# Sums of squares of the first layer's input taken from feature-major chunks, and a first tile and chunk loaded and split in halves

## The chip, the cores and the metric

The kernel runs on one core of a Trainium2 chip. The metric is the device time of one execution in microseconds (us), as the median of several runs. The engines are named as the profile names them: PE (TensorE, matrix multiplications; PEld is its weight load), DVE (VectorE), ACT (ScalarE), POOL (GpSimd) and SP (SyncE, which here only issues transfers).

## The reference, cut to what matters

Two layers, each over 256 tokens with 2048 features in float32. Everything starts with an RMS norm of the input, whose result goes through one wide projection:

```python
def rms_norm(x, gain):
    xf = x.astype(jnp.float32)
    y = xf * lax.rsqrt(jnp.mean(xf * xf, axis=-1, keepdims=True) + EPS)
    return (y * gain.astype(jnp.float32)).astype(x.dtype)
...
    for layer in range(DEPTH):
        h = rms_norm(x, norm_g[layer])
        proj = jnp.einsum("bsd,de->bse", h, w_in[layer])
        q, k, v, g_att, glu_a, glu_b, g_conv = jnp.split(proj, SPLIT_POINTS, axis=-1)
        q = apply_rope(rms_norm(q.reshape(B, S, N_HEADS, HEAD_DIM), q_norm_g[layer]), cos, sin)
        k = apply_rope(rms_norm(k.reshape(B, S, N_HEADS, HEAD_DIM), k_norm_g[layer]), cos, sin)
...
        conv = conformer_conv(glu_a, glu_b, dw_kernel[layer], dw_bias[layer], conv_ln_g[layer],
                              conv_ln_b[layer], w_pw[layer])
...
        y = jnp.einsum("bse,ed->bsd", jnp.concatenate([att_y, conv_y], axis=-1), w_out[layer])
        x = x + y
```

The factor of a token, one over the root of its mean square, is a number for each row of the projection. The kernel therefore multiplies the plain input (times the gain) with the weights first and applies that factor, `rx`, when a result leaves PSUM.

## The kernel before

**Products.** All wide projections run as one list of groups, one for each 512 output columns. A group is 8 tiles of 256 rows by 512 columns of weights. Every float32 operand is split into a rounded part and a rest: weights from `raw` into `whi` (ACT, line 229) and `wlo` (DVE, line 230), the stationary input into `sthi` (ACT) and `stlo` (DVE). A tile then takes 12 multiplications on PE (two halves of rows, two halves of tokens, three products, lines 616 to 618). Four `raw` buffers are filled by SP in the order of the tiles; a load of tile i+4 waits until the split of tile i has read the buffer. Four buffers hold split tiles, so the split of tile i+4 waits until PE has used tile i.

**Input.** The first layer's input comes feature-major from `x_t` in four chunks `Y[0]` to `Y[3]` (512 features by 256 tokens each), which `first_chunk` splits into `sthi` and `stlo`. Chunk c serves tiles 2c and 2c+1 of every group. The token-major input comes too, in four chunks `A[c]` from `x`, loaded one after another from the list `later`; `x_square` squares each on ACT with a sum along the row, and after the fourth a reduction on DVE and two small operations on POOL (`rsqrt`) give `rx`.

**The rest in between.** Everything that isn't a product is a task of `Filler`: pieces of work that a planner puts between the tiles, by priority and by costs and due times written in the code. The planner runs when the program is built; what it decides is a fixed order of instructions on each engine. The first group is glu_b: its results leave PSUM as `Sigmoid(rx * ps)` on ACT (line 308). The second is glu_a, whose results DVE multiplies with it; PE then transposes the product (line 256), and the convolution starts on DVE. Results of group g-2 have to be out before group g begins.

**POOL's own list.** After the identity matrix POOL issues the load of `mask` and, in `rope_tables`, makes four tables for rotary positions: for each it issues one load of a table and two of a gain row (`gbc`), waits for them, and multiplies (line 588). These are needed first by the group q, after four other groups.

The lines that the change touches, and the start of the program, are these:

Of the kernel before, what the change touches and what calls it, by code (L numbers as in the profile page):

```python
# [16 lines left out]
D = 2048  # L17
# [16 lines left out]
R_RAW, R_SPLIT = 4, 4  # L34
AHEAD = 3

WARM = 14


class Need:  # L40
# [105 lines left out]
def trunk(ctx: ExitStack, tc: tile.TileContext, x, w_in, q_norm_g, k_norm_g, w_pw, w_out, x_t, gains, params,  # L146
# [69 lines left out]
    def load(i):  # L216
        if i >= len(tiles):
            return
        g, s = tiles[i]
        _, _, _, w, row, col, _ = groups[g]  # L220
        r = row + s * KS * 128
        nc.sync.dma_start(raw[i % R_RAW], w[r:r + KS * 128, col:col + CH].rearrange("(k p) c -> p k c", p=128))
        loaded[i] = max(loaded.get(i - 1, 0), halved.get(i - R_RAW, 0) + 2.0) + 1.5

    def split(i):
        if i >= len(tiles):
            return
# [46 lines left out]
    def filled(s, c):  # L274
        vacant[s][c] = False
        ready[s][c] = True

    def first_chunk(c):

        yield Need(A=1.5, V=1.6)  # L280
        p = Y[c].rearrange("p (i s) -> p i s", i=4)
        for i in range(4):
            S.activation(st_hi[0][c][:, i], p[:, i], AF.Copy, scale=ng[:, 4 * c + i:4 * c + i + 1])  # L283
        for i in range(4):
            V.scalar_tensor_tensor(st_lo[0][c][:, i], p[:, i], ng[:, 4 * c + i:4 * c + i + 1],  # L285
                                   st_hi[0][c][:, i].bitcast(F32), op0=ALU.mult, op1=ALU.subtract)
# [7 lines left out]
    def x_square(l, c):  # L294
        yield Need(A=1.4)
        for tt in range(2):
            S.activation(junk, A[c][:, tt], AF.Square, accum_out=ssx[:, tt, c:c + 1])
        flag("x", l, c)
        if all(("x", l, k) in flags for k in range(4)):
            yield Need(V=0.1, G=0.6)  # L300
            V.tensor_reduce(rsc, ssx, axis=mybir.AxisListType.X, op=ALU.add)
            rsqrt(rx, rsc, 1.0 / D, 2)
            flag("rx", l)

    def ev_glu_b(l, j, ps):
        yield Need(0, has("glu", l, j - 1) if j else has("rx", l), A=1.2)
# [55 lines left out]
    def ln_square(l, j):  # L362
        yield Need(V=1.2)
        y = Y[j].rearrange("p (c s) -> p c s", c=4)
        V.tensor_add(y, y, nmean[:, None, :].to_broadcast([128, 4, SEQ]))
        yield Need(0, has("sq", l, j - 2) if j >= 2 else has("rope", l, NCH - 1, "k"), A=1.0)
        sq = Dt[1 + j % 2].rearrange("p t e -> p (t e)")
        S.activation(sq, Y[j], AF.Square)  # L368
        for h in range(2):
            yield Need(0, has("sq", l, j - 1) if j else None, G=1.3)  # L370
            half_sq = sq[:, h * CH:(h + 1) * CH]
            if j == 0 and h == 0:
                G.tensor_copy(ssum, half_sq)
            else:
                G.tensor_add(ssum, ssum, half_sq)  # L375
        flag("sq", l, j)
        if j < NCH - 1:
            return
        yield Need(1, P=0.2)
        ps = fill.bank()  # L380
        for tt in range(2):
            for i in range(2):
                T.matmul(ps[:, 2 * tt:2 * tt + 2], ssum[:, i * SEQ + tt * 128:i * SEQ + tt * 128 + 128],
                         ones[:, :2], start=(i == 0), stop=(i == 1))
        yield Need(V=0.2, G=1.5)
        V.tensor_copy(rsc, ps[:, 0:4:2])
        fill.free(ps)
        rsqrt(rstd, rsc, 1.0 / D, 2)
        G.tensor_copy(rbc, rstd[:, :, None].to_broadcast([128, 2, 128]))
        yield Need(1, P=0.5)  # L390
        ps = fill.bank()
        for tt in range(2):
            T.matmul(ps[:, tt * 128:tt * 128 + 128], rbc[:, tt], ident, start=True, stop=True)
        yield Need(A=0.4)
        S.activation(nmean, ps[:, :SEQ], AF.Copy)
        fill.free(ps)
        for k in range(NCH):
            fill.add(ln_silu(l, k), 4, fill.now[4])
# [162 lines left out]
    for i in range(WARM):  # L561
        T.matmul(acc[3], junk[:, :128], junk, start=True, stop=True)
    S.dma_start(ng, gains)
    S.dma_start(Y[0], x_t[:, 0])
    load(0)
    load(1)
    nc.sync.dma_start(Y[1], x_t[:, 1])
    load(2)
    nc.sync.dma_start(Y[2], x_t[:, 2])
    load(3)  # L570
    later = [(Y[3], x_t[:, 3], None)]
    later += [(A[c], x[0, :, c * CH:(c + 1) * CH].rearrange("(t p) e -> p t e", p=128), c) for c in range(NCH)]
    later.append((prm, params, None))
    make_identity(nc, ident)
    V.memset(half, -0.5)
    V.memset(ones, 1.0)
# [10 lines left out]
                                bass.AP(tensor=src.tensor, offset=src.offset, ap=[[0, 128], [1, 64]]))  # L587
                G.tensor_mul(rope[nm + part], rope[nm + part], gbc[:, None, :].to_broadcast([128, 2, DH]))

    for c in range(NCH):  # L590
        fill.add(first_chunk(c), 0)
    split(0)


    users = {"glu_b": ev_glu_b, "glu_a": ev_glu_a, "v": ev_v, "g_conv": ev_g_conv, "g_att": ev_g_att,
# [3 lines left out]
    for i, (g, s) in enumerate(tiles):  # L599
        l, nm, j, _, _, _, st = groups[g]  # L600
        c = s * KS // 4
        fill.until(lambda: ready[st][c])
        if s == 0 and g >= 2:
            fill.until(has("ev", *groups[g - 2][:3]))
        for a in range(i + AHEAD if i else 1, i + AHEAD + 1):
            split(a)
        ps = [acc[(2 * g + tt) % 4] for tt in range(2)]
        hi, lo = whi[i % R_SPLIT], wlo[i % R_SPLIT]
        order = [(kk, tt) for kk in range(KS) for tt in range(2)]
        if s == NSTEP - 1:  # L610
            order.sort(key=lambda o: o[1])
        for kk, tt in order:
            k = s * KS + kk
            tok = slice(tt * 128, tt * 128 + 128)
            xh, xl = st_hi[st][c][:, k % 4, tok], st_lo[st][c][:, k % 4, tok]
            T.matmul(ps[tt], xh, hi[:, kk], start=(k == 0), stop=False)  # L616
            T.matmul(ps[tt], xh, lo[:, kk], start=False, stop=False)  # L617
            T.matmul(ps[tt], xl, hi[:, kk], start=False, stop=(k == KT - 1))  # L618
        fill.use([("P", 2.6)], halved[i])
        if later and (i == 0 or i % 2):  # L620
            dst, src, c = later.pop(0)
            nc.sync.dma_start(dst, src)
            if c is not None:
                fill.add(x_square(0, c), 3, fill.t["P"] + 4.0)
        if i == NSTEP:
            G.dma_start(mask, log_count)
            rope_tables(0)
        if s % 2 and j == NCH - 1 and nm in last[st]:
            ready[st][c], vacant[st][c] = False, True
        if s == NSTEP - 1:  # L630
            fill.add(users[nm](l, j, ps), 0, fill.t["P"])
            if nm == "o_att" and j == NCH - 1 and l + 1 < DEPTH:
                rope_tables(l + 1)
        fill.run()
# [52 lines left out]
```

## Time and profile before

| what | before |
|---|---|
| median of 3 runs | 1862.9 us (1860.91 to 1862.95) |
| the profiled execution, its own time | 1864.42 us |
| its span in the profile | 1862.6 us |
| busy: PE, DVE, ACT, POOL | 1848.9, 1392.2, 989.0, 139.8 us |
| mean granted clock of PE, as a share of full speed | 0.998 |
| moved by DMA | 352.06 MB, mean 189 GB/s |

The span is the time from the first to the last instruction of the program; the execution's own time has 1.8 us more around it. Busy times of different engines lie beside each other and don't add up to the span.

### The profile page before, as it was taken

To read this page: it belongs to the slowest core of one execution; us is meant where nothing else is said; L and a number is where in the kernel's file an instruction comes from. 1 tells how busy PE (TensorE), PEld (TensorE's weight loads), DVE (VectorE), ACT (ScalarE), POOL (GpSimd) and SP (SyncE) were. 2 spreads that over 40 slices of the span, in tenths; PEclk is the share of its full clock that TensorE was granted. 3 is DMA by queue.
4 is the path that set the end of the run, shared out by engine and by line. 5 is a ranking of instruction groups with operands and counts; after the bars stand their busy time and mean duration, and the time that the engine had idled before them with its cause. 6 is when DMAs were issued, how large, how long until landed. Compare 5 with 4: busy or idle time off the path is not lost.

```text
span 1862.6 us, 23725 instructions
## 1 busy us (share of the span) xinstructions
PE 1848.9 (99%) x8490; PEld 1536.0 (82%) x8490; DVE 1392.2 (75%) x2157; ACT 989.0 (53%) x1559; POOL 139.8 (8%) x153
## 2 busy tenths in 40 slices
PE   8999999999999999999999999999999999999999
PEld 5788888888888888888888888888888888888887
DVE  5678889788889876556558888797887998755554
ACT  5565564554654456445444655646556445644542
POOL 2010100100110141000000101002000102100000
PEclk9999999999999999999999999999999999999999
DMA  8665656656566676556666656565565666666564
GB/s 268 218 184 168 180 179 180 183 167 190 175 179 193 190 225 203 193 189 191 208 203 192 186 162 184 160 197 183 162 183 167 193 194 190 213 204 194 180 204 147
DMA packets 181527, 352.06 MB, mean 189 GB/s; under 512 B 11248, under 2 KB 11248, under 8 KB 181408
## 3 DMA queue, kind: packets, MB, share of 16 engines
q1 hardware_dynamic: 179584, 347.19, 61.3%
q0 software_dynamic: 960, 1.77, 0.6%
q8 instruction: 66, 1.08, 0.2%
q10 hardware_dynamic: 864, 1.59, 0.2%
q14 instruction: 53, 0.43, 0.1%
HBM read 346.31 MB, written 4.19 MB: 188 GB/s over the span
## 4 chain that ended last, share of the span: by engine, by line
PE 97%; DMA 2%; ACT 0%; issue 0%; DVE 0%; SPq 0%; POOL 0%; ACTq 0%; DVEq 0%
PE acc L616 31%; PE acc L618 31%; PE acc L617 31%; PE ax L256 2%; DMA a<-in_x 1%; DMA raw<-in_w_in 1%; PE ax L465 1%; PE ax L482 1%; PE ax L490 0%; PE ax L491 0%; PE ax L489 0%; PE ax L464 0%; DMA y<-in_x_t 0%; ACT whi L229 0%; DVE wlo L230 0%
## 5 line engine op out<-in xcount | busy, mean ns | idle before, releaser
L230 DVE TENSOR_TENSOR wlo<-raw,whi 128x1024 fp32r<-128x1024 f32 x640 | 792.6, 1247 | 413.5 <-ACT whi L229 407.4
L229 ACT ACTIVATE whi<-raw 128x1024 fp32r<-128x1024 f32 x640 | 675.3, 1063 | 657.7 <-PE acc L618 466.3
L616 PE MATMUL acc<-whi,sthi 128*128 128x512 f32 x2560 | 1005.5, 393 | 6.0 <-ACT sthi L283 5.4
L617 PE MATMUL acc<-wlo,sthi 128*128 128x512 f32 x2560 | 997.8, 390 | 2.3 <-DVE wlo L230 2.3
L618 PE MATMUL acc<-whi,stlo 128*128 128x512 f32 x2560 | 998.2, 390 | 0.0
L616 PEld LDWEIGHTS acc<-whi,sthi 128*128 128x128 f32 x2560 | 481.6, 188 | 105.6 <-ACT sthi L283 6.3
L618 PEld LDWEIGHTS acc<-whi,stlo 128*128 128x128 f32 x2560 | 481.2, 188 | 101.5 <-DVE stlo L285 1.0
L617 PEld LDWEIGHTS acc<-wlo,sthi 128*128 128x128 f32 x2560 | 481.6, 188 | 100.9 <-DVE wlo L230 3.2
L339 DVE SCALAR_TENSOR_TENSOR y<-ut,prm,y 128x256 f32<-128x256 f32 x960 | 408.6, 483 | 0.0
L427 POOL TENSOR_SCALAR qr<-qss 128x8 f32<-128x8 f32 x16 | 3.2, 198 | 696.8 <-ACT junk L424 696.8
L347 POOL TENSOR_TENSOR ysum<-ysum,y 128x256 f32<-128x256 f32 x30 | 36.5, 1218 | 240.8 <-DVE y L339 133.5
L424 ACT ACTIVATE junk<-acc,rx 128x128 bf16<-128x128 f32 x128 | 47.1, 368 | 8.4 <-PE acc L618 4.8
L434 ACT ACTIVATE d<-acc,qr 128x128 f32<-128x128 f32 x128 | 34.8, 383 | 15.8 <-POOL qr L429 15.8
L267 ACT ACTIVATE sthi<-ax,prm 128x256 fp32r<-128x256 f32 x64 | 25.1, 476 | 30.7 <-PE ax L256 30.7
L269 DVE SCALAR_TENSOR_TENSOR stlo<-ax,prm,sthi 128x256 fp32r<-128x256 f32 x64 | 26.5, 475 | 14.4 <-ACT sthi L267 14.4
L455 ACT ACTIVATE c<-ax 128x512 f32<-128x512 f32 x32 | 17.4, 596 | 33.6 <-PE ax L256 33.6
L478 ACT ACTIVATE sm<-sm,smm 128x128 f32<-128x128 f32 x64 | 28.2, 443 | 6.6 <-DVE smm L473 6.6
L375 POOL TENSOR_TENSOR ssum<-ssum,d 128x512 f32<-128x512 f32 x14 | 28.5, 2033 | 6.5 <-ACT d L368 5.6
L428 POOL TENSOR_TENSOR qr<-qr,half 128x8 f32<-128x8 f32 x16 | 26.3, 1642 | 1.3
L256 PEld LDWEIGHTS ax<-ident,d 128*128 128x128 f32 x192 | 22.4, 140 | 3.2
L256 PE MATMUL ax<-ident,d 128*128 128x128 f32 x192 | 24.9, 273 | 0.0
L424 ACT ACTIVATION_READ_ACCUMULATOR junk<-acc,rx 128x1 f32 x128 | 24.7, 193 | 0.0
(105 smaller groups left out, 659.3 us busy)
## 6 DMA issues: line engine op xcount, KB each, us to landing
raw<-in_w_in SPq DMA_DIRECT2D x448, 512.0 KB, 4.1
raw<-in_w_out SPq DMA_DIRECT2D x128, 512.0 KB, 4.7
raw<-in_w_pw SPq DMA_DIRECT2D x64, 512.0 KB, 4.6
a<-in_x SPq DMA_DIRECT2D x8, 512.0 KB, 6.0
xs<-a SPq DMA_DIRECT2D x4, 512.0 KB, 6.5
a<-xs SPq DMA_DIRECT2D x4, 512.0 KB, 6.6
y<-in_x_t SPq DMA_DIRECT2D x3, 512.0 KB, 12.4
out<-a SPq DMA_DIRECT2D x4, 256.0 KB, 6.0
```

The lines of the kernel that those rows point to most:

```text
L229: S.activation(hi, a, AF.Copy)
L230: V.tensor_sub(wlo[i % R_SPLIT], a, hi.bitcast(F32))
L256: T.transpose(banks[b][:, i * SEQ + tt * 128:i * SEQ + tt * 128 + 128], src[:, tt, e:e + 128], ident)
L339: V.scalar_tensor_tensor(y[:, c], u[:, c, k:k + SEQ], w[:, c, l * CW + k:l * CW + k + 1], y[:, c], op0=ALU.mult, op1=ALU.add)
L347: G.tensor_add(ysum, ysum, y[:, c])
L375: G.tensor_add(ssum, ssum, half_sq)
L424: S.activation(junk[:, :DH], ps[tt][:, h * DH:(h + 1) * DH], AF.Square, scale=rx[:, tt:tt + 1], accum_out=qss[:, tt, h:h + 1])
L434: S.activation(n[:, tt, h * DH:(h + 1) * DH], ps[tt][:, h * DH:(h + 1) * DH], AF.Copy, scale=qr[:, tt, h:h + 1])
L478: S.activation(s[:, cs], s[:, cs], AF.Exp, bias=m[:, tt:tt + 1], scale=-1.0, accum_out=lsum[:, tt:tt + 1])
L616: T.matmul(ps[tt], xh, hi[:, kk], start=(k == 0), stop=False)
L617: T.matmul(ps[tt], xh, lo[:, kk], start=False, stop=False)
L618: T.matmul(ps[tt], xl, hi[:, kk], start=False, stop=(k == KT - 1))
```

## The change

The first layer's sums of squares are taken from the feature-major chunks, and the token-major input isn't loaded for them. Per chunk, ACT squares 128x1024 numbers into a free buffer (`x_square_first`), POOL adds the two halves into `ssum`, and after the fourth chunk PE multiplies `ssum` with ones (4 small multiplications, `token_sums`), DVE copies two columns, and `rsqrt` follows as before. The four loads of `A` are gone. The first weight tile and the first input chunk are loaded in halves, alternating, all on SP's queue, and split half by half (`split_first`); the first tile's multiplications stand in an order that begins with what comes first. 9 warm-up multiplications stand where 14 stood. The parameters (`prm`) are loaded after tile 7.

```diff
-WARM = 14
+WARM = 9
...
+        src = w[r:r + KS * 128, col:col + CH].rearrange("(k p) c -> p k c", p=128)
+        for kk in range(KS) if i == 0 else [slice(0, KS)]:
+            nc.sync.dma_start(raw[i % R_RAW][:, kk], src[:, kk])
+            if i == 0:
+                x_load(0, 2 * kk, 2 * kk + 2)
...
+    def split_first():
+
+        for kk in range(KS):
+            for k in (2 * kk, 2 * kk + 1):
+                S.activation(*first_hi(0, k), AF.Copy, scale=ng[:, k:k + 1])
+                if k == 2 * kk:
+                    S.activation(whi[0][:, kk], raw[0][:, kk], AF.Copy)
+            V.tensor_sub(wlo[0][:, kk], raw[0][:, kk], whi[0][:, kk].bitcast(F32))
+            for k in (2 * kk, 2 * kk + 1):
+                first_lo(0, k)
+        fill.use([("A", 2.9), ("V", 3.0)], 4.5)
+        halved[0] = 7.0
+        filled(0, 0)
+        fill.add(x_square_first(0), 3, 7.0)
+        load(R_RAW)
...
         filled(0, c)
+        fill.add(x_square_first(c), 3, fill.now[4])
...
+    def x_square_first(c):
+
+        yield Need(0, has("sqx", c - 2) if c >= 2 else None, A=1.0)
+        sq = Dt[1 + c % 2].rearrange("p t e -> p (t e)")
+        S.activation(sq, Y[c], AF.Square)
+        yield from add_squares(sq, c, "sqx")
+        if c == NCH - 1:
+            yield from token_sums()
+            rsqrt(rx, rsc, 1.0 / D, 2)
+            flag("rx", 0)
+
+    def add_squares(sq, j, *name):
+        for h in range(2):
+            yield Need(0, has(*name, j - 1) if j else None, G=1.3)
+            half_sq = sq[:, h * CH:(h + 1) * CH]
+            if j == 0 and h == 0:
+                G.tensor_copy(ssum, half_sq)
+            else:
+                G.tensor_add(ssum, ssum, half_sq)
+        flag(*name, j)
+
+    def token_sums():
+
+        yield Need(1, P=0.2)
+        ps = fill.bank()
+        for tt in range(2):
+            for i in range(2):
+                T.matmul(ps[:, 2 * tt:2 * tt + 2], ssum[:, i * SEQ + tt * 128:i * SEQ + tt * 128 + 128],
+                         ones[:, :2], start=(i == 0), stop=(i == 1))
+        yield Need(V=0.2, G=1.5)
+        V.tensor_copy(rsc, ps[:, 0:4:2])
+        fill.free(ps)
...
-    S.dma_start(Y[0], x_t[:, 0])
     load(0)
     load(1)
-    nc.sync.dma_start(Y[1], x_t[:, 1])
+    x_load(1)
     load(2)
-    nc.sync.dma_start(Y[2], x_t[:, 2])
     load(3)
-    later = [(Y[3], x_t[:, 3], None)]
-    later += [(A[c], x[0, :, c * CH:(c + 1) * CH].rearrange("(t p) e -> p t e", p=128), c) for c in range(NCH)]
-    later.append((prm, params, None))
+    x_load(2)
...
-    for c in range(NCH):
-        fill.add(first_chunk(c), 0)
-    split(0)
+    split_first()
+    for c in range(1, NCH):
+        fill.add(first_chunk(c), 0, 5.0 + 4.0 * c)
...
             split(a)
+            if a == 1:
+                x_load(3)
...
-        if later and (i == 0 or i % 2):
-            dst, src, c = later.pop(0)
-            nc.sync.dma_start(dst, src)
-            if c is not None:
-                fill.add(x_square(0, c), 3, fill.t["P"] + 4.0)
+        if i == NSTEP - 1:
+            nc.sync.dma_start(prm, params)
         if i == NSTEP:
             G.dma_start(mask, log_count)
             rope_tables(0)
```

The planner puts the new work at these places. POOL's list of instructions right behind the identity matrix, before (`gbc` is the gain row of a table):

```order
L626 DMA mask<-in_log_count 128x384
L583 DMA ropeqa<-in_rope_cos 128x2x128
L586 DMA gbc<-in_q_norm_g 128x64 x2
L588 TENSOR_TENSOR ropeqa<-ropeqa,gbc 128x256
L583 DMA ropeqb<-in_rope_sin 128x2x128
```

The same place now (`d_108` and `d_109` hold the squares of chunks 0 and 2, and of 1 and 3):

```order
L351 COPY ssum<-d_108 128x512
L353 TENSOR_TENSOR ssum<-ssum,d_108 128x512
L353 TENSOR_TENSOR ssum<-ssum,d_109 128x512 x2
L353 TENSOR_TENSOR ssum<-ssum,d_108 128x512 x2
L671 DMA mask<-in_log_count 128x384
L627 DMA ropeqa<-in_rope_cos 128x2x128
L630 DMA gbc<-in_q_norm_g 128x64 x2
L632 TENSOR_TENSOR ropeqa<-ropeqa,gbc 128x256
```

The sums of three chunks stand ahead of the mask and the tables now. The end of POOL's tables before, up to the two operations that make `rx`:

```order
L583 DMA ropekb<-in_rope_sin 128x2x128
L586 DMA gbc<-in_k_norm_g 128x64 x2
L588 TENSOR_TENSOR ropekb<-ropekb,gbc 128x256
L247 TENSOR_SCALAR rx<-rsc 128x2
L248 TENSOR_TENSOR rx<-rx,half 128x2
```

The same place now:

```order
L627 DMA ropekb<-in_rope_sin 128x2x128
L630 DMA gbc<-in_k_norm_g 128x64 x2
L632 TENSOR_TENSOR ropekb<-ropekb,gbc 128x256
L353 TENSOR_TENSOR ssum<-ssum,d_109 128x512 x2
L270 TENSOR_SCALAR rx<-rsc 128x2
L271 TENSOR_TENSOR rx<-rx,half 128x2
```

The sum of the fourth chunk stands behind all four tables. PE's list where tile 9 (the second tile of the group glu_a) ends and tile 10 begins, before:

```order
L616 MATMUL acc_156<-whi_94,sthi_65 128x512
L617 MATMUL acc_156<-wlo_98,sthi_65 128x512
L618 MATMUL acc_156<-whi_94,stlo_73 128x512
L616 MATMUL acc_155<-whi_95,sthi_66 128x512
L617 MATMUL acc_155<-wlo_99,sthi_66 128x512
L618 MATMUL acc_155<-whi_95,stlo_74 128x512
```

The same place now:

```order
L665 MATMUL acc_156<-whi_94,sthi_65 128x512
L665 MATMUL acc_156<-wlo_98,sthi_65 128x512
L665 MATMUL acc_156<-whi_94,stlo_73 128x512
L362 MATMUL ax_157<-ones,ssum 128x2 x4
L665 MATMUL acc_155<-whi_95,sthi_66 128x512
L665 MATMUL acc_155<-wlo_99,sthi_66 128x512
```

Four small multiplications, whose operand is POOL's finished `ssum`, stand between the tiles. On ACT `rx` is used at the same place as before: behind the split of tile 13. ACT's list at the start, before, with the semaphores that each row waits for (one of a DMA is named DMAHW; `ng` is the first row's load, of the gains):

```order
L563 DMA ng<-in_gains 128x32
L564 DMA y_81<-in_x_t 128x1024
L229 ACT_TABLE_LOAD
L229 ACTIVATE whi_93<-raw_89 128x1024 [waits DMAHW1_49]
L283 ACTIVATE sthi_65<-y_81,ng 128x256 [waits DMAHW2_49,DMAHW0_49]
```

The same place now:

```order
L611 DMA ng<-in_gains 128x32
L245 ACT_TABLE_LOAD [waits DMAHW2_49]
L245 ACTIVATE sthi_65<-y_81,ng 128x256 [waits DMAHW0_49]
L247 ACTIVATE whi_93<-raw_89 128x512 [waits DMAHW1_49]
L245 ACTIVATE sthi_65<-y_81,ng 128x256
L245 ACTIVATE sthi_65<-y_81,ng 128x256 [waits DMAHW4_49]
```

The load of the activation table comes behind the arrival of the gains, and a quarter of the input chunk is split ahead of the first half of the weights.

## Rows read from the trace of the kernel before

**Rows 1.** Waits of PE over the whole run: us in total, times, longest.

```profile
PE acc L616 <- ACT sthi L283: 5.4, 2, 3.2
```

**Rows 2.** Timeline of PE: start us, us, line, operation [idle before <-releaser].

```profile
9.00 0.55 PE L616 MATMUL acc<-whi,sthi 128*128 128x512 f32 x1 [2.18 <-ACT sthi L283]
...
10.20 0.63 PE L616 MATMUL acc<-whi,sthi 128*128 128x512 f32 x1
...
10.63 0.63 PE L617 MATMUL acc<-wlo,sthi 128*128 128x512 f32 x1
...
19.58 0.80 PE L616 MATMUL acc<-whi,sthi 128*128 128x512 f32 x1 [3.24 <-ACT sthi L283]
...
61.43 0.39 PE L616 MATMUL acc<-whi,sthi 128*128 128x512 f32 x1
...
66.19 0.39 PE L616 MATMUL acc<-whi,sthi 128*128 128x512 f32 x1
...
66.88 1.04 PE L256 MATMUL ax<-ident,d 128*128 128x128 f32 x8
```

**Rows 3.** One stretch: PE, PEld, DVE, ACT, POOL busy, then granted clock, DMA.

```profile
10.00:12.00 2.00, 2.00 (x6) 1.51 (x6) 1.54 (x3) 1.10 (x2) 0.00 (x0) 0.50 0.95 239
```

**Rows 4.** Timeline of POOL, first layer.

```profile
1.43 0.78 POOL L626 DMA_DIRECT2D mask<-in_log_count  x1
...
21.73 0.75 POOL L583 DMA_DIRECT2D ropeka<-in_rope_cos  x1
22.48 1.08 POOL L586 DMA_DIRECT2D gbc<-in_k_norm_g  x2
28.20 0.74 POOL L588 TENSOR_TENSOR ropeka<-ropeka,gbc 128x256 f32<-128x256 f32 x1 [4.64 <-DMA gbc<-in_k_norm_g]
...
36.97 0.73 POOL L588 TENSOR_TENSOR ropekb<-ropekb,gbc 128x256 f32<-128x256 f32 x1 [6.25 <-DMA gbc<-in_k_norm_g]
54.27 0.18 POOL L247 TENSOR_SCALAR rx<-rsc 128x2 f32<-128x2 f32 x1 [16.56 <-DVE rsc L301]
```

**Rows 5.** Timeline of POOL, the last table of the second layer.

```profile
711.82 1.86 POOL L588 TENSOR_TENSOR ropekb<-ropekb,gbc 128x256 f32<-128x256 f32 x1 [3.72 <-DMA gbc<-in_k_norm_g]
```

**Rows 6.** Timeline of ACT, first layer.

```profile
0.72 0.45 ACTq L563 DMA_DIRECT2D ng<-in_gains  x1
...
1.73 1.28 ACT L229 ACT_TABLE_LOAD   x1 [1.73 <-issue]
...
18.07 1.06 ACT L229 ACTIVATE whi<-raw 128x1024 fp32r<-128x1024 f32 x1 [1.53 <-DMA raw<-in_w_in]
19.04 1.69 ACT L283 ACTIVATE sthi<-y,ng 128x256 fp32r<-128x256 f32 x4
20.63 1.04 ACT L229 ACTIVATE whi<-raw 128x1024 fp32r<-128x1024 f32 x1
...
56.45 3.90 ACT L229 ACTIVATE whi<-raw 128x1024 fp32r<-128x1024 f32 x4
```

**Rows 7.** Line 368, ACT's squares for layer_norm: duration ns min/median/max.

```profile
L368 ACT ACTIVATE d<-y x8: 1068/1073/1079, 653.9 to 1588.3; 128x1024 f32<-128x1024 f32 x8
```

**Rows 8.** Instructions on `ssum`, both layers: duration ns min/median/max.

```profile
L383 PE MATMUL ax<-ones,ssum x16: 166/251/251, 679.9 to 1601.3; 128*128 128x2 f32 x16
L375 POOL TENSOR_TENSOR ssum<-ssum,d x14: 1296/2154/2168, 655.7 to 1591.7; 128x512 f32<-128x512 f32 x14
L373 POOL COPY ssum<-d x2: 614/616/617, 655.0 to 1575.8; 128x512 f32<-128x512 f32 x2
```

**Rows 9.** DMA: issues by line (KB, us to landing), then the landing of `gbc`.

```profile
ng<-in_gains ACTq DMA_DIRECT2D x1, 16.0 KB, 3.8
...
DMA to landing us min/median/max: 3.2/5.0/10.2
```

**Rows 10.** Timeline of DVE in the second layer's first normalisation, POOL adding squares beside it.

```profile
652.60 1.22 DVE L230 TENSOR_TENSOR wlo<-raw,whi 128x1024 fp32r<-128x1024 f32 x1
...
656.66 4.55 DVE L230 TENSOR_TENSOR wlo<-raw,whi 128x1024 fp32r<-128x1024 f32 x2
```

More of the change, by code (lines that the diff above doesn't have):

```diff
@@ L221, in load, with x_load @@
         r = row + s * KS * 128
-        nc.sync.dma_start(raw[i % R_RAW], w[r:r + KS * 128, col:col + CH].rearrange("(k p) c -> p k c", p=128))
+        src = w[r:r + KS * 128, col:col + CH].rearrange("(k p) c -> p k c", p=128)
[3 more added lines that the diff above has]
+                x_load(0, 2 * kk, 2 * kk + 2)
         loaded[i] = max(loaded.get(i - 1, 0), halved.get(i - R_RAW, 0) + 2.0) + 1.5
+    def x_load(c, a=0, b=4):
+        nc.sync.dma_start(Y[c][:, a * SEQ:b * SEQ], x_t[:, c, a * SEQ:b * SEQ])
     def split(i):
@@ L276, in filled, with first_hi, first_lo @@
         ready[s][c] = True
+    def first_hi(c, i):
+        return st_hi[0][c][:, i], Y[c][:, i * SEQ:(i + 1) * SEQ]
+    def first_lo(c, i):
+        hi, src = first_hi(c, i)
+        V.scalar_tensor_tensor(st_lo[0][c][:, i], src, ng[:, 4 * c + i:4 * c + i + 1], hi.bitcast(F32),
+                               op0=ALU.mult, op1=ALU.subtract)
     def first_chunk(c):
         yield Need(A=1.5, V=1.6)
-        p = Y[c].rearrange("p (i s) -> p i s", i=4)
         for i in range(4):
-            S.activation(st_hi[0][c][:, i], p[:, i], AF.Copy, scale=ng[:, 4 * c + i:4 * c + i + 1])
+            S.activation(*first_hi(c, i), AF.Copy, scale=ng[:, 4 * c + i:4 * c + i + 1])
         for i in range(4):
-            V.scalar_tensor_tensor(st_lo[0][c][:, i], p[:, i], ng[:, 4 * c + i:4 * c + i + 1],
-                                   st_hi[0][c][:, i].bitcast(F32), op0=ALU.mult, op1=ALU.subtract)
+            first_lo(c, i)
         filled(0, c)
+        fill.add(x_square_first(c), 3, fill.now[4])
     def x_chunk(l, c):
@@ L368, in ln_square @@
         S.activation(sq, Y[j], AF.Square)
[L369 to L376, printed above, removed]
+        yield from add_squares(sq, j, "sq", l)
         if j < NCH - 1:
             return
[L379 to L387, printed above, removed]
+        yield from token_sums()
         rsqrt(rstd, rsc, 1.0 / D, 2)
@@ L611, in trunk @@
             order.sort(key=lambda o: o[1])
-        for kk, tt in order:
+        products = [(kk, tt, n) for kk, tt in order for n in range(3)]
+        if i == 0:
+            products.sort(key=lambda o: (o[0], o[2]))
+        for kk, tt, n in products:
             k = s * KS + kk
@@ L615, in trunk @@
             xh, xl = st_hi[st][c][:, k % 4, tok], st_lo[st][c][:, k % 4, tok]
-            T.matmul(ps[tt], xh, hi[:, kk], start=(k == 0), stop=False)
-            T.matmul(ps[tt], xh, lo[:, kk], start=False, stop=False)
-            T.matmul(ps[tt], xl, hi[:, kk], start=False, stop=(k == KT - 1))
+            T.matmul(ps[tt], xl if n == 2 else xh, lo[:, kk] if n == 1 else hi[:, kk],
+                     start=(k == 0 and n == 0), stop=(k == KT - 1 and n == 2))
         fill.use([("P", 2.6)], halved[i])
-        if later and (i == 0 or i % 2):
-            dst, src, c = later.pop(0)
-            nc.sync.dma_start(dst, src)
-            if c is not None:
-                fill.add(x_square(0, c), 3, fill.t["P"] + 4.0)
+        if i == NSTEP - 1:
+            nc.sync.dma_start(prm, params)
         if i == NSTEP:
```

## The prediction

> **What bounds the kernel now.** I read the waits of PE first. Over the whole run PE waits for other engines only a few times; the largest sum is 5.4 us in two waits, for the split input [rows 1]. Then I read PE's timeline to see where its waits lie: all before 60 us. The first product starts at 9.00, a second wait of 3.24 us ends at 19.58, and at 66.88 stand the first transposes [rows 2]. From there to the end PE has work without a gap, so whatever moves 66.88 moves the end by as much, and the case is decided before it.
>
> At full clock a product follows the one before it every 0.2267 us: from 61.43 to 66.19 there are 21 steps [rows 2]. Seventeen tiles of 12 products stand ahead of the transposes: 204 x 0.2267 = 46.25 us. 66.88 - 9.00 - 46.25 = 11.6 us are lost behind the first product, and 9.00 us ahead of it. That is all that an edit of the start could win. After a pause the products are slower: 10.20 and 10.63 lie 0.43 us apart [rows 2], and the granted clock of that stretch is 0.50 [rows 3], the lower of the two levels, 1.2 GHz. Eight such products cost 8 x 0.2 = 1.6 us more.
>
> The third view is POOL's timeline. POOL does one thing after another: a table for rotary positions takes 0.75 for its load's issue, 1.08 for the two gain rows' issue, 4.64 waiting for them and 0.74 for the multiplication, 7.2 us in all, and the four of them and the mask keep POOL from 1.43 to 37.7 us [rows 4]. Before, that delays nobody: `rx` is asked of POOL at 54.27 only, after 16.56 us of idleness [rows 4].
>
> **The change part by part.**
>
> *The first halves.* The activation table's load, which ran at 1.73, stands behind the arrival of the gains now: issued at 0.72 [rows 6], landed 3.8 us later [rows 9], at 4.5; with the 1.28 us of the load [rows 6] ACT begins at 5.8. A quarter of the input chunk (a fourth of 1.59, the step of four, 19.04 to 20.63 [rows 6]) and half a weight tile (between 0.4, the step of a 256-column quarter, and 0.97, a fourth of the 3.90 that four full ones take [rows 6]; I take 0.6, half and something fixed) give a first product at 6.8 instead of 9.00: 2.2 us won. The five warm-up products that are gone end earlier in a time when PE waits anyway; if the clock starts lower for it, that is within the 1.6 us, which I leave as they are.
>
> *The third tile.* Before, ACT came to the split of tile 3 when its weights landed at 18.07 [rows 6], the seventh of seven half-megabyte loads; the second chunk was split behind it, and so PE waited until 19.58. Now it is the sixth, and POOL's loads are no longer beside it. A sixth or seventh of the way less gives 0.7 + 17.3 x 6/7 = 15.6; without POOL's loads I take 14.5, bounds 13 and 18. PE would wait about 1 us where it waited 3.24.
>
> *The squares.* The four loads of `A`, their eight squarings and the wait for the last are gone, and `rx` would be early. In exchange ACT does four squares of 1.07 us [rows 7] and POOL eight operations on `ssum`. What matters is where POOL does the last two. The order shows the sums of chunks 0 to 2, then the mask and all four tables, then the sum of chunk 3; and on PE the four multiplications of `ssum` between tiles 9 and 10. PE takes its products in the order of its list, so tile 10 and all behind it wait for POOL's tables. The sum for that:
>
> 1. ACT from tile 3's split (14.5) to the end of chunk 2's square: five weight splits, three chunks and two squares lie ahead (5 x 0.97 + 3 x 1.59 + 2 x 0.98 = 11.6), then the square itself, 1.07: 27.2.
> 2. POOL adds chunk 2: two operations. Before, such an addition takes 2.154 us in the median and 1.296 at least [rows 8]. DVE splits weights at the time, so I take the median: 31.5. The earlier chunks' sums (0.62 for the copy, 2.15 each otherwise) fit between the squares.
> 3. The mask's issue, 0.78 [rows 4]: 32.3.
> 4. Four tables. Two at 7.2 as above, while loads still run; two at 6.3, with the shortest wait that a table had, 3.72 [rows 5], since by about 45 us every buffer is full and SP's loads stop. Together 27.0: 59.3. Bounds: with the shortest landing of a gain row, 3.2 [rows 9], less its 0.54 of issue, all four take 4 x (0.75 + 1.08 + 2.7 + 0.73) = 21.0; with the longest late wait, 6.25 [rows 4], 4 x 8.8 = 35.
> 5. The two additions of chunk 3. By then DVE has nothing to split, for tile 14 needs a buffer that PE's tile 10 frees. I take the least duration, 2 x 1.30 = 2.6; with the median it would be 4.3: 61.9.
> 6. Four multiplications with ones, 0.25 [rows 8] and their weight loads: 0.9. Tile 10 begins at 62.8.
> 7. Seven tiles to the transposes: 84 x 0.2267 = 19.04, and 1.6 for the clock after so long a pause: 83.4.
>
> That is 83.4 - 66.88 = 16.5 us later. `rx` itself (a copy, a small power) comes some 4 us after the sums, and ACT needs it only when PE comes to tile 14, 10.9 us on: hidden. PE would have come to tile 10 by about 15 + 8 x 2.72 = 37 to 39, so its wait there is some 23 us.
>
> On step 5 the additions' two durations matter. In the second layer, while POOL adds squares, two of DVE's subtractions take 4.55 us where one alone takes 1.22 [rows 10]: both are slowed. The Trainium skill (SBUF — State Buffer, "SBUF: two separate sides") says that an operation of DVE with two inputs and one of GpSimd exclude each other at a shared port for a whole instruction. The trace agrees, with 2.28 for 1.22. By this rule the squares on POOL would also slow DVE's splits between 17 and 31 us, against the change; by the rows about (2.28 - 1.22) x 6 = 6 us of DVE's time, whose share on PE ends before 40 us, inside the wait for POOL.
>
> *What costs nothing.* `prm` is loaded later, but the convolution that reads it begins after the transposes. The longer list of ACT (four squares for eight squarings) is shorter in time. Were the wait for POOL gone, DVE's slowing would show with up to some 4 us.
>
> **The sum.** Span: 1862.6 + 16.5 = 1879.1. The profiled execution took 1.8 us more than its span, 1864.42; it was slower than the median of the runs, 1862.9. I put the change on the median: 1879.4, so 1879.
>
> **The rivals.**
>
> *The change does what it says, and the tables are not in the way.* Were `ssum` ready when PE comes to tile 10, the losses behind a first product at 6.8 would be the clock (1.6), the third tile (1.0), DVE beside POOL (2.0, half of its up to 4) and the small multiplications (0.9): 6.8 + 46.25 + 5.5 = 58.6 at the transposes, 8.3 us earlier: 1855. For that the four tables would have to be done by 34. Their issues and multiplications alone, without any wait, take 0.78 + 4 x 2.56 = 11.0 us from 31.5 on, so with the order as it is this would need chunk 2 squared some 10 us earlier too. Break-even is tile 10 at about 46.2, with `ssum` whole at 45.3; the least of all bounds (step 1 at 25.7, additions of 1.3, tables of 21.0) gives 52.7. Chance 0.04; no change 0.02.
>
> *The tables are quick in the quiet.* With waits of 2.7 throughout, tile 10 begins at 56.8 and the time is 1873. If the waits in the quiet were shorter still, 1870. For it: SP's loads stop. Against: in neither layer is a wait under 3.72 seen. Chance 0.10 for under 1873. The Trainium skill (DMA: Bandwidth & Descriptors, "Anatomy of one DMA — SWDGE (gpsimd) path") gives a fixed cost of about 2.0 us for a small transfer of this kind. By that the estimate is waits of about 1.5 us after the last issue and some 1868; no row here shows one so short.
>
> *The tables are slow.* At 8.8 each and late weights at the start (18 in step 1): 8 + 3.5 more, 1891. For it: the last table of the first layer waited 6.25 beside SP's loads. Chance 0.08 for more than 1887.
>
> **How the numbers follow.** The forecast, a wait for POOL with tables between the bounds, has 0.76 within 1873 to 1887; the low end is taken down to 1871 since the quiet case is the likelier of the two tails. A change under 0.2% (3.7 us) can't be told from none by such runs. All cases but the first rival are slower by more: slower 0.94, same 0.02, faster 0.04.
>
> **What the profile of the changed kernel would show.** Right: the largest wait of PE is that of the multiplications with ones for POOL's `ssum`, once, 20 to 26 us; POOL's last two additions begin behind the fourth table, near 59, and take about 1.3 us each; the first product stands near 6.8, the third tile's near 15. Wrong: if that wait is under 8 us, POOL's sums were earlier than the order says, and the first rival holds; if the wait is as said but the transposes lie under 78, step 4's waits were too long; if PE has new waits after 83 us, the shift isn't the whole of it.

## The result, and the profile after

| what | before | after |
|---|---|---|
| median (4 runs each, on the same chip) | 1862.9 us (1860.91 to 1864.51) | 1880.9 us (1879.75 to 1882.54) |
| the profiled execution, its own time | 1864.42 us | 1879.75 us |
| its span | 1862.6 us | 1878.0 us |
| mean granted clock of PE | 0.998 | 0.994 |
| moved by DMA | 352.06 MB | 349.97 MB |

The changed kernel takes 1.0095 of the time before (95% interval 1.0082 to 1.0108). It is slower by 0.8 to 1.1%, 18.0 us by the medians and 15.4 us by the two profiled spans.

The first view is again the waits of PE: engine, line, what it waited for, then us in total, times, and the longest. After the change:

```profile
PE ax L362 <- POOL ssum L353: 20.9, 1, 20.9
PE acc L610 <- DVE junk L608: 1.4, 1, 1.4
PE acc L665 <- ACT whi L247: 1.2, 1, 1.2
PE acc L665 <- DVE wlo L237: 1.2, 1, 1.2
PE acc L665 <- DVE stlo L306: 0.5, 1, 0.5
```

One wait of 20.9 us leads the list. It is that of the multiplications with ones for POOL's `ssum`, and it comes once. The 5.4 us for the split input [rows 1] are gone; in their place stand 1.2 at the first product and 0.5 at the third tile.

The second view is PE's timeline after the change, at the places of [rows 2]:

```profile
6.70 1.22 PE L665 MATMUL acc<-whi,sthi 128*128 128x512 f32 x2 [1.24 <-ACT whi L247]
...
15.16 0.50 PE L665 MATMUL acc<-whi,stlo 128*128 128x512 f32 x1 [0.47 <-DVE stlo L306]
...
30.04 0.50 PE L665 MATMUL acc<-wlo,sthi 128*128 128x512 f32 x1 [1.22 <-DVE wlo L237]
...
37.91 0.39 PE L665 MATMUL acc<-whi,stlo 128*128 128x512 f32 x1
59.16 1.86 PE L362 MATMUL ax<-ones,ssum 128*128 128x2 f32 x8 [20.87 <-POOL ssum L353]
60.89 0.77 PE L665 MATMUL acc<-whi,sthi 128*128 128x512 f32 x1
...
64.87 0.52 PE L665 MATMUL acc<-whi,sthi 128*128 128x512 f32 x1
...
82.06 1.04 PE L279 MATMUL ax<-ident,d 128*128 128x128 f32 x8
```

The first product is 2.3 us earlier, the third tile's wait (tile 2, as tiles are counted from 0) is 0.47 us where it was 3.24, and PE is done with ten tiles at 38.3. Then it stands for 20.9 us, and the transposes begin at 82.06 where they began at 66.88.

What POOL did meanwhile, in its own timeline (first layer):

```profile
20.59 7.99 POOL L353 TENSOR_TENSOR ssum<-ssum,d 128x512 f32<-128x512 f32 x4 [2.44 <-ACT d L339]
28.51 0.78 POOL L671 DMA_DIRECT2D mask<-in_log_count  x1
29.30 0.74 POOL L627 DMA_DIRECT2D ropeqa<-in_rope_cos  x1
30.03 1.11 POOL L630 DMA_DIRECT2D gbc<-in_q_norm_g  x2
38.37 0.72 POOL L632 TENSOR_TENSOR ropeqa<-ropeqa,gbc 128x256 f32<-128x256 f32 x1 [7.24 <-DMA gbc<-in_q_norm_g]
...
45.45 0.72 POOL L632 TENSOR_TENSOR ropeqb<-ropeqb,gbc 128x256 f32<-128x256 f32 x1 [4.59 <-DMA gbc<-in_q_norm_g]
...
50.66 0.72 POOL L632 TENSOR_TENSOR ropeka<-ropeka,gbc 128x256 f32<-128x256 f32 x1 [2.71 <-DMA gbc<-in_k_norm_g]
...
55.83 0.72 POOL L632 TENSOR_TENSOR ropekb<-ropekb,gbc 128x256 f32<-128x256 f32 x1 [2.68 <-DMA gbc<-in_k_norm_g]
56.52 2.59 POOL L353 TENSOR_TENSOR ssum<-ssum,d 128x512 f32<-128x512 f32 x2
```

Three chunks are summed at 28.5. The mask and the four tables then hold POOL until 56.5, and only behind them stand the last two additions, 2.6 us of work for which PE has been waiting since 38.3. Of those 28 us POOL spends 17.2 in four waits for gain rows.

Stretches of the same execution (their length, then PE, PEld, DVE, ACT and POOL busy, the granted clock, the share of DMA, GB/s) show how the stop spreads:

```profile
40.00:50.00 10.00, 0.00 (x0) 0.00 (x0) 2.62 (x3) 3.05 (x3) 3.36 (x6) 0.56 0.85 255
50.00:60.00 10.00, 0.84 (x4) 0.84 (x5) 0.00 (x0) 0.00 (x0) 5.69 (x7) 0.50 0.12 20
60.00:70.00 10.00, 10.00 (x36) 8.27 (x37) 1.65 (x3) 3.39 (x4) 0.91 (x2) 0.74 0.07 8
```

From 50 to 60 us ACT and DVE do nothing either, all split tiles and `raw` buffers being full, so the loads stop too (20 GB/s). The granted clock has fallen to 0.50 by then, and PE pays for it behind the wait.

### The profile page after: what moved, and what is told of

The parts are those of the page before. It is cut to its first block, busy times and chain, and to the rows that moved or that the text cites. A ratio compares the mean times of both kernels' runs of the same rounds, so it can differ in the third digit from the quotient of the medians.

```text
span 1878.0 us, 23730 instructions
## 1 busy us (share of the span) xinstructions
PE 1848.6 (98%) x8493; PEld 1537.6 (82%) x8493; DVE 1397.2 (74%) x2158; ACT 987.5 (53%) x1548; POOL 151.7 (8%) x161
## 2 busy tenths in 40 slices
DMA packets 180599, 349.97 MB, mean 186 GB/s; under 512 B 11216, under 2 KB 11216, under 8 KB 180480
## 4 chain that ended last, share of the span: by engine, by line
PE 97%; DMA 1%; POOL 1%; ACT 0%; issue 0%; SPq 0%; DVE 0%; POOLq 0%
PE acc L665 91%; PE ax L279 2%; PE ax L513 1%; DMA gbc<-in_q_norm_g 1%; PE ax L530 1%; POOL ssum L353 1%; DMA raw<-in_w_in 0%; PE ax L538 0%; PE ax L539 0%; PE ax L537 0%; PE ax L512 0%; DMA gbc<-in_k_norm_g 0%; PE ax L362 0%; POOL gbc L630 0%; ACT whi L236 0%
## 5 line engine op out<-in xcount | busy, mean ns | idle before, releaser
L290 ACT ACTIVATE sthi<-ax,prm 128x256 fp32r<-128x256 f32 x64 | 25.1, 475 | 30.7 <-PE ax L279 30.7
L353 POOL TENSOR_TENSOR ssum<-ssum,d 128x512 f32<-128x512 f32 x21 | 40.1, 1908 | 9.3 <-ACT d L431 5.6
L526 ACT ACTIVATE sm<-sm,smm 128x128 f32<-128x128 f32 x64 | 28.2, 442 | 6.6 <-DVE smm L521 6.6
L279 PE MATMUL ax<-ident,d 128*128 128x128 f32 x192 | 24.9, 273 | 0.0
```

Source lines behind the costliest of these rows:

```text
L279: T.transpose(banks[b][:, i * SEQ + tt * 128:i * SEQ + tt * 128 + 128], src[:, tt, e:e + 128], ident)
L526: S.activation(s[:, cs], s[:, cs], AF.Exp, bias=m[:, tt:tt + 1], scale=-1.0, accum_out=lsum[:, tt:tt + 1])
```

## The experiments

Every kernel was timed beside the kernel before on the same chip, and that one's median was 1862.7 to 1863.2 us on each of them. One table first, since it holds for all. The third number column is the 27th product, the first that needs the remainders of the second chunk; the last is the span less the moment of the first transposes.

| kernel | median us | first product | 27th product | transposes | span from there |
|---|---|---|---|---|---|
| before | 1862.9 | 9.00 | 20.84 | 66.88 | 1795.7 |
| after | 1880.9 | 6.70 | 15.16 | 82.06 | 1795.9 |
| e1, tables last | 1857.6 | 6.77 | 15.24 | 59.21 | 1795.9 |
| e2, tables' loads at once | 1870.4 | 6.82 | 16.03 | 72.73 | 1796.0 |
| e3, ones behind tile 13 | 1872.1 | 6.91 | 15.36 | 75.80 | 1795.9 |
| e4, halves alone | 1861.0 | 7.61 | 18.25 | 64.28 | 1795.6 |
| e5, squares, whole start | 1857.1 | 7.97 | 15.63 | 58.12 | 1796.0 |
| e6, e1 and later squares | 1854.8 | 6.78 | 15.90 | 57.29 | 1795.9 |
| e7, e6 and 14 warm-ups | 1854.7 | 7.11 | 15.83 | 57.24 | 1796.0 |
| e8, e5 and later squares | 1855.0 | 8.06 | 15.39 | 56.80 | 1796.0 |

From the first transposes to the end all ten take 1795.6 to 1796.0 us. The case is decided ahead of that point, and each difference of medians can be looked for there.

**e1: the tables behind tile 16.** Theory: POOL's tables ahead of its last sum are the whole loss. The rival is that something else of the change (squares beside splits, ones on PE) costs as well.

```diff
-        if i == NSTEP:
+        if i == 2 * NSTEP:
             G.dma_start(mask, log_count)
             rope_tables(0)
```

> Edit: the mask and the four tables are issued after tile 16 instead of tile 8, so that on POOL they stand behind all sums of squares and behind rx; nothing else differs from the changed kernel. Theory (PE waits in its own list for POOL's sums, and POOL's sums wait for the tables): the 20.9 us wait goes away entirely, tile 10 begins near 39, the transposes stand at 58 to 59.5 and the median is 1853 to 1857, faster than before the change. Rival (the squares are late for another reason: ACT's list, or POOL's additions beside DVE): the wait shrinks only in part, the transposes stay above 66.9 and the median above 1862.

Measured: 1857.6 us, 0.9972 of before (0.9961 to 0.9982). PE's timeline of e1:

```profile
31.20 0.50 PE L665 MATMUL acc<-wlo,sthi 128*128 128x512 f32 x1 [2.29 <-DVE wlo L237]
...
39.26 0.95 PE L362 MATMUL ax<-ones,ssum 128*128 128x2 f32 x8
...
59.21 1.04 PE L279 MATMUL ax<-ident,d 128*128 128x128 f32 x8
```

The multiplications with ones wait for nothing, and take 0.95 us at full clock. The place of the tables alone is worth 23.3 us, and makes of a loss a gain. It is more than the wait of 20.9 us, for with the wait the slow clock behind it goes as well. That it came out 0.6 us above the range points at the one wait that is left, 2.29 us for a split by DVE at tile 7. POOL's and DVE's timelines of e1 lie beside each other there:

```profile
20.67 11.62 POOL L353 TENSOR_TENSOR ssum<-ssum,d 128x512 f32<-128x512 f32 x6 [2.45 <-ACT d L339]
```

```profile
23.09 5.85 DVE L306 SCALAR_TENSOR_TENSOR stlo<-y,ng,sthi 128x256 fp32r<-128x256 f32 x4
28.86 6.78 DVE L237 TENSOR_TENSOR wlo<-raw,whi 128x1024 fp32r<-128x1024 f32 x4
```

Four remainders that take 1.66 us elsewhere take 5.85 while POOL adds squares. ACT had split tile 7's weights at 22.98; DVE came to them at 28.86 only, so it was DVE that PE waited for. e6 asks whether POOL's additions are the cause.

**e2: the tables' loads issued in one go.** Theory: the time in the tables is waiting, row by row; with a buffer for each gain row the twelve loads wait together. They stay ahead of the last sum.

```diff
-                G.dma_start(rope[nm + part], tab.rearrange("(t p) d -> p t d", p=128))
...
-                G.tensor_mul(rope[nm + part], rope[nm + part], gbc[:, None, :].to_broadcast([128, 2, DH]))
+        for (n, g, tab, swap), gbc in zip(todo, gbcs):
+            G.dma_start(rope[n], tab.rearrange("(t p) d -> p t d", p=128))
...
+        for (n, g, tab, swap), gbc in zip(todo, gbcs):
+            G.tensor_mul(rope[n], rope[n], gbc[:, None, :].to_broadcast([128, 2, DH]))
```

> Edit: the tables stay ahead of the fourth chunk's sum, but have a gain row's buffer each; all twelve loads are issued in a row and the four multiplications follow. Theory (the tables cost what their four waits one behind the other cost): POOL needs 0.8 + 7.3 for issues, one wait of 5 to 8 us and 2.9 for the multiplications, 16 to 19 instead of 27.4 us; PE's wait falls from 20.9 to 10 to 13 us and the median to 1869 to 1873. Rival (the wait comes from something other than the tables, or POOL's loads go one after another anyway): the median stays within 2 us of 1881.

Measured: 1870.4 us, 1.0038 (1.0024 to 1.0052). POOL's timeline of e2:

```profile
30.17 0.74 POOL L629 DMA_DIRECT2D ropeqa<-in_rope_cos  x1
...
37.07 0.71 POOL L629 DMA_DIRECT2D ropekb<-in_rope_sin  x1 [1.48 <-DMA gbc<-in_q_norm_g]
...
46.52 0.72 POOL L635 TENSOR_TENSOR ropekb<-ropekb,t 128x256 f32<-128x256 f32 x1 [1.52 <-DMA t<-in_k_norm_g]
47.20 2.60 POOL L354 TENSOR_TENSOR ssum<-ssum,d 128x512 f32<-128x512 f32 x2
```

The tables take 17.0 us in place of 27.2, and PE waits 10.7 in place of 20.9: us for us. What went is waiting: POOL's waits in the tables (three of them at issues, three at multiplications) come to 6.7 us, where they were 17.2, while issues and multiplications take about 10 us in either kernel.

**e3: the ones later on PE.** Theory: it is the place of the multiplications with ones in PE's list that turns POOL's lateness into PE's. POOL is left as it is; PE may do tiles 10 to 13 first.

```diff
-        yield Need(1, P=0.2)
+        yield Need(1, lambda: tile_now[0] >= 13, P=0.2)
```

> Edit: POOL's list as in the changed kernel, tables included; only the multiplications with ones stand behind tile 13 on PE instead of tile 9. Theory (what costs is PE's own list, not that rx is late): the sums are ready at the same 59 us, PE does four more tiles (10.9 us) ahead of them, its wait falls from 20.9 to about 10, the transposes stand near 71 and the median is 1869 to 1872. Rival (a late rx holds up the first group's way out on ACT, whatever PE's list): the wait turns up elsewhere on PE and the median stays within 3 us of 1881.

Measured: 1872.1 us, 1.0046 (1.0032 to 1.006). PE's largest wait of e3, then POOL's last additions:

```profile
PE ax L363 <- POOL ssum L354: 13.9, 1, 13.9
```

```profile
54.51 0.72 POOL L633 TENSOR_TENSOR ropeka<-ropeka,gbc 128x256 f32<-128x256 f32 x1 [5.08 <-DMA gbc<-in_k_norm_g]
...
60.62 2.59 POOL L354 TENSOR_TENSOR ssum<-ssum,d 128x512 f32<-128x512 f32 x2
```

The direction is as expected, the size is not: since PE goes on, the weights' loads go on as well (from 50 to 55 us 216 GB/s are moved, 39 in after), the third table waits 5.08 where it waited 2.71, and the last additions begin at 60.62 where they began at 56.52. Four microseconds of the gain are given back.

**e4: the halves alone.** The start in halves, with the token-major input and the tables as before.

```diff
-        fill.add(x_square_first(0), 3, 7.0)
-        fill.add(x_square_first(c), 3, fill.now[4])
+    later = [(A[c], x[0, :, c * CH:(c + 1) * CH].rearrange("(t p) e -> p t e", p=128), c) for c in range(NCH)]
+    later.append((prm, params, None))
```

> Edit: only the first half of the change: first tile and chunk in halves, 9 warm-up products; the squares come from the token-major input as before, with its four loads after tiles 1, 3, 5 and 7, and the tables run on POOL from the start as before. Theory (the start gains by itself and the squares on POOL lose): first product near 6.8, transposes at 59 to 63, median 1855 to 1859. Rival (the start's gain is eaten, since the chain of four loads of A and their squares sets rx): transposes at 65 to 67, median 1861 to 1863.

Measured: 1861.0 us, 0.9988 (0.9979 to 0.9997), under 0.2% from before. ACT's timeline of e4:

```profile
15.48 1.06 ACT L236 ACTIVATE whi<-raw 128x1024 fp32r<-128x1024 f32 x1 [0.28 <-DMA raw<-in_w_in]
...
30.05 0.63 ACT L325 ACTIVATE junk<-a 128x512 bf16<-128x512 f32 x1 [4.17 <-DMA a<-in_x]
...
47.79 0.63 ACT L325 ACTIVATE junk<-a 128x512 bf16<-128x512 f32 x1 [2.31 <-DMA a<-in_x]
```

The time lies between the two. The start wins 2.6 us at the 27th product (18.25 for 20.84), as much as tile 3's weights are split earlier (15.48 for 18.07 [rows 6]), and all of it is still there at the transposes, against the rival. It is no more for two reasons that the table and these rows show. POOL's loads stay in the start: the first product comes at 7.61, not near 6.8 as expected, and tile 3's split at 15.48 (6.70 and 12.39 in after). And ACT goes on standing in its list for the four loads of `A`, 11.8 us in four waits of which the first and the last are shown; behind such stops come PE's five waits between 32 and 57 us, 3.4 us in all.

**e5: the squares with the start as before.** First tile and chunk whole, 14 warm-ups, feature-major squares, tables last.

```diff
-WARM = 9
+WARM = 14
...
-    split_first()
-    for c in range(1, NCH):
-        fill.add(first_chunk(c), 0, 5.0 + 4.0 * c)
+    for c in range(NCH):
+        fill.add(first_chunk(c), 0)
+    split(0)
```

> Edit: only the second part of the change, with the tables out of the way: the start is that of before (first tile whole, first chunk whole on ACT's queue, 14 warm-up products), the squares come from the feature-major chunks, and mask and tables are issued after tile 16. Theory (start and squares gain apart from each other, and what they gain adds up less than fully, since the four loads of A hold tiles 11 to 14 whatever the start does): first product at 8 to 9, second chunk's tile near 17 since POOL's loads are gone from the start, transposes at 61 to 63, median 1857.5 to 1860. Rival (the gain of the kernel with the tables last is the start's): transposes at 65 to 67, median 1861 to 1863.

Measured: 1857.1 us, 0.9968 (0.9956 to 0.998). That is e1's time without the halves: beside the squares the halves add nothing, against the theory, and the transposes come at 58.12, earlier than the 61 to 63 expected. The reason is in the arrival of the weights of tile 3, behind whose split ACT has the second chunk's, in ACT's timeline of e5:

```profile
12.86 1.06 ACT L233 ACTIVATE whi<-raw 128x1024 fp32r<-128x1024 f32 x1 [1.58 <-DMA raw<-in_w_in]
```

Before it stood at 18.07 [rows 6], with the same order of loads on SP's queue and the same list on ACT up to there. What is gone from the start is POOL's table loads. The stretch from 10 to 15 us, first before and then in e5, shows it in the last column (GB/s) at the same share of DMA:

```profile
10.00:15.00 5.00, 5.00 (x17) 3.95 (x17) 1.90 (x3) 1.10 (x2) 1.17 (x2) 0.73 0.97 327
```

```profile
10.00:15.00 5.00, 4.69 (x19) 3.01 (x17) 3.49 (x3) 3.27 (x6) 0.00 (x0) 1.00 1.03 383
```

e4 and after are the second such pair: both start in halves, e4 with POOL's tables beside it and after without, and tile 3's weights are split at 15.48 and 12.39.

**e6: the squares 10 us later.** Theory: POOL's additions slow DVE's splits of the start; planned later, they meet DVE when it has slack.

```diff
-        fill.add(x_square_first(0), 3, 7.0)
+        fill.add(x_square_first(0), 3, 7.0 + 10.0)
...
-        fill.add(x_square_first(c), 3, fill.now[4])
+        fill.add(x_square_first(c), 3, fill.now[4] + 10.0)
```

> Edit: the kernel with the tables last, and every chunk's square is due 10 us later to the planner, so that ACT's squares stand one to two tiles later and the multiplications with ones behind tile 11 instead of 9. Theory (the 2.3 us that PE still waits at tile 7 come from POOL's additions beside DVE's subtractions): that wait goes or falls under 1 us, DVE's four remainders of the fourth chunk take 1.7 to 4 instead of 5.85 us, and the median is 1854.5 to 1857.5. Rival (that wait is for late weights, or the contention only moves to the next tiles): another wait of 1 to 3 us appears and the median stays at 1857 to 1859.

Measured: 1854.8 us, 0.9954 (0.9942 to 0.9967). DVE's and POOL's timelines of e6:

```profile
22.15 1.66 DVE L306 SCALAR_TENSOR_TENSOR stlo<-y,ng,sthi 128x256 fp32r<-128x256 f32 x4
```

```profile
28.82 10.84 POOL L353 TENSOR_TENSOR ssum<-ssum,d 128x512 f32<-128x512 f32 x6 [2.09 <-ACT d L339]
```

The last chunk's remainders take 1.66 us again, tile 7's wait is gone, and the transposes come 1.9 us before e1's. POOL's additions still slow DVE, but later, where it has idle time between its splits, and PE doesn't wait for it there; alone such a split takes 1.22:

```profile
30.47 2.12 DVE L237 TENSOR_TENSOR wlo<-raw,whi 128x1024 fp32r<-128x1024 f32 x1 [1.49 <-ACT whi L236]
```

**e7 and e8: what the start is worth now.** e7 is e6 with 14 warm-ups in place of 9; e8 is e5 with the later squares of e6, the whole start of before.

```diff
-WARM = 9
+WARM = 14
```

> The changed kernel with tables last, squares planned 10 us later, and 14 warm-up products as before the change, in place of 9. Theory (PE's start is paced by the arrival and the split of the third and fourth weight tile, so a first product 1.2 us earlier or a higher clock in the first 12 products only lengthens the wait at that tile): the product with the third tile's remainders stands at 15.2 to 16.0 as with 9 warm-ups, the transposes at 56.5 to 57.8, the median at 1854 to 1856, not to be told from the 1854.8 of the same kernel with 9. Rival (the warm-ups end at about 7.5, behind the moment when the first half is split, so they delay the first product by 0.7 us and all that follows with it): transposes at 58, median 1855.5 to 1856.5.

> The start of the kernel before (first tile and chunk whole, 14 warm-ups) with feature-major squares planned 10 us later and the tables last. Theory (the halves win nothing that PE can keep, because the third tile's chunk is split at about 15 in either; feature-major squares, the tables' place and the squares' time make all of the gain): first product near 8.0, the third tile's remainders at 15.2 to 16.2, transposes at 56.5 to 58, median 1854 to 1856. Rival (the halves are worth their 1.2 us once nothing else waits): transposes 1 to 1.5 us later than with halves, median 1856 to 1857.5.

Measured: e7 1854.7 us, 0.9955 (0.9943 to 0.9968); e8 1855.0 us, 0.996 (0.9947 to 0.9974). Both theories hold. PE's timeline of e8:

```profile
8.06 0.50 PE L659 MATMUL acc<-whi,sthi 128*128 128x512 f32 x1 [1.39 <-ACT sthi L310]
...
15.39 0.50 PE L659 MATMUL acc<-whi,stlo 128*128 128x512 f32 x1 [0.53 <-DVE stlo L303]
```

Its first product is 1.3 us behind that of e6, its 27th is not behind at all: all of them meet at the third tile, whose chunk comes behind tile 3's weights and isn't split before about 15. e6, e7 and e8 can't be told apart, and all three are faster than the kernels before and after the change.

## Why the prediction was right, point by point

The forecast was 1879 (1871 to 1887), slower, and 1880.9 was measured. Its mechanism is the one that the profile shows, and e1 to e3 take it apart: without the tables ahead of the last sum the loss is gone, with shorter tables it shrinks by as much, and with the ones later on PE it shrinks. That the number came so near is in part luck, since several terms were off and their errors cancel.

*The first halves.* First product at 6.8 forecast, 6.70 measured. The term for the gains was luck: I took them for what holds up the table's load, at 4.5. They landed 3.0 us behind their issue, at 3.7; the load waited for the first half of the input chunk, and ran at 4.32:

```profile
4.32 1.28 ACT L245 ACT_TABLE_LOAD   x1 [4.32 <-DMA y<-in_x_t]
```

In e4, where the gains landed as early but that half later, it ran at 5.23. The first eight products stand 0.43 us apart or a little more, and from the first to the 27th 2.1 us are lost beside the wait of 0.47; I had kept 1.6 for that.

*The third tile.* ACT came to it at 12.39, not 14.5, outside my bounds of 13 to 18: POOL's loads in the start had cost more than I gave them, 5.2 us (e5) where I took 1.1 off for them. That tile 3's weights are the sixth load and no longer the seventh is worth nothing: as the seventh, in e5, they are split at 12.86, as the sixth, in e6, at 13.13. PE's wait was 0.47 for 1.

*Steps 1 and 2.* The timeline of ACT after the change has tile 3's split and the square of chunk 2 at:

```profile
12.39 1.06 ACT L236 ACTIVATE whi<-raw 128x1024 fp32r<-128x1024 f32 x1 [0.28 <-DMA raw<-in_w_in]
...
23.84 1.05 ACT L339 ACTIVATE d<-y 128x1024 f32<-128x1024 f32 x1
```

The square ends at 24.9 (27.2 forecast), 12.5 us behind the start of tile 3's split as in the sum (12.7). The three chunks' sums were done at 28.5 and not 31.5: 2.3 us of that are the earlier square, the rest the additions. Of POOL's row of four the first, of chunk 1, takes 3.67 us, and chunk 2's two are done 3.7 us behind their square, where I took 2 x 2.154 [rows 8].

*Steps 3 and 4.* From the mask's end to the last table 27.2 us; 27.0 forecast. The sum was right and its parts were not, so it was right by luck. I took two tables of 7.2 and two of 6.3; they took 9.7, 7.1, 5.2 and 5.2. The first, beside the weights' loads, waited 7.24 us. The kernel before has a longer one, for its own first table, which I had left out as belonging to the crowded start, and that was the mistake:

```profile
13.83 0.74 POOL L588 TENSOR_TENSOR ropeqa<-ropeqa,gbc 128x256 f32<-128x256 f32 x1 [9.78 <-DMA gbc<-in_q_norm_g]
```

The last two waited 2.7, the value of the quiet rival and of my lower bound. The first two took 2.4 us more than the sum has, the last two 2.2 less, and the errors cancel. The price of the Trainium skill (DMA: Bandwidth & Descriptors, "Anatomy of one DMA — SWDGE (gpsimd) path"), about 2.0 us fixed, by which I had estimated waits of 1.5 us and 1868, was too low here: in the quietest stretch, at 20 GB/s, the wait behind the last issue was still 2.68 us, and no landing of a gain row was under 3.0:

```profile
DMA to landing us min/median/max: 3.0/4.4/7.6
```

*Step 5.* Two additions alone: 2.59 for 2.6.

*Step 6.* The multiplications with ones took 1.86 us for 0.9. The price was that of full clock, which e1 confirms (0.95 at a granted clock of 1.00); here PE had stood for 20 us and the granted clock was 0.50, and behind the waits of e2 and e3 they took 1.87. Half the clock for the small multiplications is the term that I left out.

*Step 7.* Nine products stand 0.43 us apart or more until 64.87, so that the pause cost some 2 us of clock, 1.6 forecast. The transposes came at 82.06 for 83.4, the shift was 15.2 us for 16.5.

*The wait* was 20.9 us, forecast at 20 to 26. Behind 82 us there is no new wait of PE, and the span grew by 15.4.

*What costs nothing, and the cover.* The wait for POOL covered what its additions do to DVE's splits, as said: after has a wait of 1.22 us at tile 7, which costs nothing there. In e1 it is 2.29, because POOL goes on with chunk 3's additions until 32.3, beside that tile's split, where in after it turns to the mask and the tables at 28.5. In e1 nothing covers it, and e6 gets 1.9 us of it back; I had put it at up to 4 us. The chain of work that ended last in after (start, us, what) gives the steps of POOL beside the four remainders:

```profile
24.33 1.38 POOL ssum L353
25.77 1.37 POOL ssum L353
27.21 1.36 POOL ssum L353
```

The remainders of the same stretch, by their line (duration ns min/median/max):

```profile
L306 DVE SCALAR_TENSOR_TENSOR stlo<-y,ng,sthi x4: 1515/1520/1525, 23.0 to 27.3; 128x256 fp32r<-128x256 f32 x4
```

One addition and one remainder are done every 1.44 us. By the Trainium skill (SBUF — State Buffer, "SBUF: two separate sides") the two engines exclude each other for a whole instruction. The trace agrees in that they go in turns, a remainder of 0.48 us (e6) being held for 1.52. It doesn't agree with the whole of both: a step of 1.44 us is less than the 1.30 [rows 8] and 0.48 of both alone, 1.78.

*The rivals.* "Does what it says, tables not in the way" was put at 1855; e1, where that is made true, gave 1857.6, and e6, with DVE disturbed only where it has slack, 1854.8. "Quick in the quiet" was right on the two tables of the quiet stretch, and lost to the slow first one. "Tables slow" was right on that one alone.

*Size.* The span grew by 15.4 us and the medians differ by 18.0. The profiled execution of before was 1.5 us above its median, that of after 1.1 below. The shift of 16.5 was 1.1 too much by the spans and 1.5 too little by the medians.

## What to carry to other kernels

When work moves to an engine that takes its list in order, read the whole list: what stands ahead of the last small operation decides, even if it is only waiting for a few rows of 256 bytes. Ask of an earlier start where its lead is next stopped, for a first product 1.3 us earlier (e6 beside e8) was worth nothing when the second chunk's split, behind tile 3's weights, set the pace. Work that is free behind a long wait has a price as soon as the wait is gone; plan it for a time when the engine that it disturbs has slack.

## What the runs showed of the hardware

- Small loads issued by POOL slow large ones beside them. Without the tables' loads in the first 20 us, 383 GB/s were moved from 10 to 15 us where it was 327, POOL's own loads included, and the seventh half-megabyte load was in use 5.2 us earlier (e5 against before). How much of this is the small packets and how much their place in the queues was not tried.
- The same small loads take longer beside the weights' loads: in after 7.24 us of waiting with 216 GB/s moved (31 to 38.4 us), 2.7 with these stopped. The rate alone doesn't give the wait: before, it was 4.64 us at 336 GB/s (23.6 to 28.2 us) and 6.25 at 227 (30.7 to 37).
- In e2 POOL's eleventh issue in a row waited 1.48 us for the landing of an earlier load of its own, though the two share no buffer, and the next two 1.38 and 1.31. Which resource it waits for was not tried.
- In after, the first eight products stand 0.43 us apart or more, as at 1.2 GHz, while the granted clock from 6 to 10 us (behind ACT's and POOL's busy time in the row below) reads 1.00. With 14 warm-ups, e5's first products stand 0.22 to 0.33 apart; but in e3, with 9 as in after, they stand 0.22 to 0.36 apart, so it isn't the number of warm-ups alone. The two views of after don't agree there, and which of them is off stays open.

```profile
6.00:10.00 4.00, 3.30 (x8) 2.59 (x9) 3.32 (x7) 3.45 (x7) 0.00 (x0) 1.00 1.01 375
```
